# Turning a norm's rows with the root on a diagonal matrix, in a two-network fp32 kernel on one core

## The chip, the cores and the metric

The kernel runs on one core of one Trainium2 chip. The core has a matrix engine (TensorE, "PE" in the profile), a vector engine (VectorE, "DVE"), a scalar engine (ScalarE, "ACT"), a general engine (GpSimd, "POOL") and an engine that here only starts transfers (SyncE, "SP"). The metric is the device time of one execution in microseconds; the figure for a kernel is the median of several runs.

## The reference

Two small networks run one after the other on the same 256 rows x of 1024 fp32 numbers. What matters here are the norms and what they feed:

```python
def rmsnorm(x, g):
    y = x * lax.rsqrt(jnp.mean(x * x, axis=-1, keepdims=True) + RMS_EPS)
    return y * g

def first_block(x, mem, ...):
    for l in range(2):
        h = rmsnorm(x, norm_mix[l])
        (u_ssm, q_lat, kv_lat, k_rope, hg_q, ..., gate_logits) = jnp.split(h @ w_in[l], ...)
        y_ssm = s5_mixer(u_ssm, ...)
        y_mla = mla_mixer(q_lat, kv_lat, ...)   # rmsnorm(q_lat, q_norm) @ w_uq, rmsnorm(kv_lat, kv_norm) @ w_ukv
        y_hg = hgrn2_mixer(hg_q, ...)           # (rmsnorm(o, g_norm) per head * silu(gate)) @ w_o
        x = x + (gated sum of the three) @ w_out[l]
        x = x + memory_cross_attention(rmsnorm(x, norm_cross[l]), ...)
        x = x + swiglu_ffn(rmsnorm(x, norm_ffn[l]), ...)
    return rmsnorm(x, norm_final)

def second_block(x, c, ...):
    for layer in range(2):
        shift, scale, gate = jnp.split(silu(c) @ w_ada[layer] + b_ada[layer], 3, axis=-1)
        h = rmsnorm(x, norm_g[layer]) * (1.0 + scale) + shift
        y = even_mixer(h, ...) if layer == 0 else odd_mixer(h, ...)   # window and sparse attention; block attention
        x = x + gate * y
    return rmsnorm(x, final_g)
```

## The kernel before

The 256 rows are two row tiles of 128 partitions (t = 0, 1). Every weight is streamed from the chip's memory in pieces of 128x512 fp32 numbers (`piece`): SP starts the transfer into `raw`, ACT rounds it to the high part `whi` (L383), and DVE subtracts to get the low part `wlo` (L384). A product in full precision is then three products of a faster fp32 type (`mm3`, L389 to L391): high by high, high by low, low by high. The activations have to stand with their features on the partitions for that, and split in the same way. So `transT_into` turns 128x128 blocks on PE with an identity matrix (L486), four blocks to a bank of PE's output memory; ACT copies the bank out as the high part and DVE subtracts for the low part (L489).

A norm before (`norm`): ACT squares both halves of a row tile with a sum per row (L469, with a read of the accumulator), POOL adds the halves up with the scale 1/1024 (L452, L456) and raises the sum to the power -1/2 (L462); this number per row is called the root here. DVE multiplies the row by root and weight at once, in two halves (L500), and the eight blocks are turned. `normer` does this for the mixer's norm of the first network's second layer, for both cross attention norms and both feed-forward norms. `mla_lat` does it for the two latents of the MLA mixer (L622 with 256 columns, L633 with 512), and `hg_out` for four heads with four roots per row (L850 by the roots, L851 by the gate). The two norms of the second network also add a shift to all rows: L1523 in its second layer, and L1550 and L1553 in its first, which is worked together with the first network's last norm and therefore multiplies a row that was normed once by a second root (`rtb`). Shift and scale come from a small product, are written to memory, and are read back with a copy on every partition (`ada_row`).

The order on each engine is not written out by hand: a scheduler places the instructions by its own estimates of their lengths and by priorities. `residual`, which adds a product to x, works it so that row tile 0 ends first; the last pieces of the weight are kept for tile 1 (they are the ones named `B` or `E` beside `whi`), so PE works the kept products of tile 1 while tile 0's norm is made by the other engines. `high_priority` brings that norm forward.

Of the kernel before, what the change touches and what calls it, by code (L numbers as in the profile page):

```python
# [13 lines left out]
ALU = mybir.AluOpType  # L14
# [3 lines left out]
P = 128  # L18
NT = 2
D = 1024  # L20
# [183 lines left out]
class Net:  # L204
# [264 lines left out]
        self.nc.scalar.activation(j[:, :n], src, AF.Square, accum_out=s)  # L469
        return s  # L470

    def transT(self, src, kt, t, tag, scale=None, slots=None):
# [4 lines left out]
        self.transT_into(src, kt, hi, lo, 0, scale)  # L477
        return hi, lo

    def transT_into(self, src, kt, hi, lo, k_at, scale=None):  # L480
        nc = self.nc
        for b in range(0, kt, 4):
            nb = min(4, kt - b)
            pt = self.trb([P, 4, P])[:, :nb]
            for j in range(nb):
                nc.tensor.transpose(pt[:, j, :], src[:, (b + j) * P:(b + j + 1) * P], self.ident)  # L486
            h, l = hi[:, k_at + b:k_at + b + nb, :], lo[:, k_at + b:k_at + b + nb, :]
            if scale is None:
                self.last_turned = nc.scalar.copy(h, pt), nc.vector.tensor_sub(l, pt, h.bitcast(F32))  # L489
            else:  # L490
                nc.scalar.mul(h, pt, scale)
                nc.vector.scalar_tensor_tensor(l, pt, scale, h.bitcast(F32), op0=ALU.mult, op1=ALU.subtract)

    def norm(self, xt, g, out=None):
# [8 lines left out]
    def into(self, T, t, xn):  # L503

        if not T:
            T.extend(self.place_rows())
        self.transT_into(xn, 8, T[0][:, :, t, :], T[1][:, :, t, :], 0)

    def normer(self, name):

        g, T = self.bcast(name, D, "gbc"), []
        return T, lambda t: self.into(T, t, self.norm(self.xs[t], g))


    def sincos(self, ang, k, s, c, sign=1.0):
# [99 lines left out]
    def mla_lat(self, l, hT, gq, gkv):  # L615
        nc = self.nc
        S = {"knT": [], "kp": [], "qnT": [], "V": []}
        pk = self.proj(hT, f"wkv{l}", 0, 8, every=1)
        for t in range(NT):
            r = self.rstd([self.ssq(pk[t][:, :256], "ssqb")], 256, "rsk")  # L620
            kn = self.t([P, 512], "w2a", bufs=2)[:, :256]
            nc.vector.scalar_tensor_tensor(kn, pk[t][:, :256], r, gkv, op0=ALU.mult, op1=ALU.mult)  # L622
            S["knT"].append(self.transT(kn, 2, t, "mk", slots=(f"Q{2 * t}", f"Q{2 * t + 1}")))
            pe = self.t([P, 32], f"kpe{t}")
            tmp = self.t([P, 2, 16], "kpet", bufs=2)
            self.rope1(pe, pk[t][:, 256:272], pk[t][:, 272:288], self.mcos[:, t, :], self.msin[:, t, :],
                       (tmp[:, 0], tmp[:, 1]), pe[:, :16], pe[:, 16:])
            S["kp"].append(pe)
        pq = self.proj(hT, f"win{l}", 0, 8, every=1)
        for t in range(NT):  # L630
            r = self.rstd([self.ssq(pq[t], "ssqa")], 512, "rsq")
            qn = self.t([P, 512], "w2a", bufs=2)
            nc.vector.scalar_tensor_tensor(qn, pq[t], r, gq, op0=ALU.mult, op1=ALU.mult)  # L633
            S["qnT"].append(self.transT(qn, 4, t, "mq", slots=(f"H{2 * t}", f"H{2 * t + 1}")))
        return S

    def mla_qkv(self, l, S):
# [196 lines left out]
    def hg_out(self, S):  # L834
        nc = self.nc
        outT = []
        for t in range(NT):
            o = self.accb([P, 4, P])
            for h in range(4):
                A = S["A"][t, h // 2]  # L840
                nc.tensor.matmul(o[:, h, :], A[0][:, h % 2, :], S["V"][t][:, h * P:(h + 1) * P], start=True, stop=t == 0)
                if t == 1:
                    nc.tensor.matmul(o[:, h, :], A[1][:, h % 2, :], S["V"][0][:, h * P:(h + 1) * P], start=False, stop=True)
            ss = self.t([P, 4], "hss", bufs=2)
            jk = self.t([P, 512], "junk", BF16)
# [6 lines left out]
            self.dump(f"hg{t}", y)  # L852
            outT.append(self.transT(y, 4, t, "gT", slots=(f"H{6 + 2 * t}", f"H{7 + 2 * t}")))
        return outT


# [642 lines left out]
            yield  # L1499

    def ada_row(self, l, i, r):
        self.nc.sync.dma_start(r, self.adad[l][:, i * D:(i + 1) * D].partition_broadcast(P).rearrange("p o n -> p (o n)"))
        return r

    def ada_rows(self, l, shift, scale):

        nc = self.nc
        self.ada_row(l, 0, shift)
        self.ada_row(l, 1, scale)
        for c in range(2):  # L1510
            cols = slice(c * 512, c * 512 + 512)
            g = self.s(f"B{c}", [P, 512])
            nc.sync.dma_start(g, self.A[f"normg{l}"][:, cols].partition_broadcast(P).rearrange("p o n -> p (o n)"))
            nc.vector.scalar_tensor_tensor(scale[:, cols], scale[:, cols], 1.0, g, op0=ALU.add, op1=ALU.mult)
        self.ada_ready = shift, scale

    def norm_ada(self, l):
        shift, g = self.ada_ready
        out = []

        def then(t):
            xn = self.norm(self.xs[t], g)
            self.nc.vector.tensor_add(xn, xn, shift)  # L1523
            self.into(out, t, xn)

        return out, then

    def norm_ada2(self, l):

        nc = self.nc  # L1530
        shift, g = self.ada_ready
        gf = self.bcast("normf", D, "gbc")
        out, rs = [], []

        def then(t):
            x = self.xs[t]
            xn = self.t([P, D], "xn")
            cols = [slice(c * 512, c * 512 + 512) for c in range(2)]

            r, q = (self.t([P, 1], n, bufs=2) for n in ("rs", "rq"))  # L1540
            for i, c in enumerate(cols):
                nc.vector.tensor_mul(xn[:, c], x[:, c], gf[:, c])
                s, u = self.ssq(x[:, c], f"ssq{i}"), self.ssq(xn[:, c], f"ssu{i}")
                nc.gpsimd.tensor_scalar(r, s, 1.0 / D, r if i else EPS, op0=ALU.mult, op1=ALU.add)
# [336 lines left out]
```

## Time and profile before

| | us |
|---|---|
| median of 3 runs | 1493.55 |
| lowest and highest run | 1491.51 and 1494.88 |
| the profiled execution | 1489.82 |
| its span, first to last instruction | 1488.0 |
| PE busy | 1404.0 (94%) |
| DVE busy | 1097.8 (74%) |
| ACT busy | 823.9 (55%) |
| POOL busy | 51.7 (3%) |
| transfers, mean | 174 GB/s |

The busy time of PE includes a modelled tail of each product, so consecutive products overlap in it: two records that start 0.23 us apart may each be shown as 0.39 long. What a product costs is therefore read from the distance of starts. The granted clock of PE was 0.990 of full speed over the span. In the timeline a row's bracket tells how long its engine was idle before it, and which instruction ended that idle time.

### The profile page before, as it was taken

To read this page: it belongs to the slowest core of one execution; us is meant where nothing else is said; L and a number is where in the kernel's file an instruction comes from. 1 tells how busy PE (TensorE), PEld (TensorE's weight loads), DVE (VectorE), ACT (ScalarE), POOL (GpSimd) and SP (SyncE) were. 2 spreads that over 40 slices of the span, in tenths; PEclk is the share of its full clock that TensorE was granted. 3 is DMA by queue.
4 is the path that set the end of the run, shared out by engine and by line. 5 is a ranking of instruction groups with operands and counts; after the bars stand their busy time and mean duration, and the time that the engine had idled before them with its cause. 6 is when DMAs were issued, how large, how long until landed. Compare 5 with 4: busy or idle time off the path is not lost.

```text
span 1488.0 us, 28521 instructions
## 1 busy us (share of the span) xinstructions
PE 1404.0 (94%) x10148; PEld 1183.6 (80%) x10148; DVE 1097.8 (74%) x2287; ACT 823.9 (55%) x1789; POOL 51.7 (3%) x135
## 2 busy tenths in 40 slices
PE   6999899999999999989999999999999899999997
PEld 5788777878899977778777778789988687767776
DVE  7886987666598887567897776588885775677656
ACT  5575555556455555485556565555544455544564
POOL 1100001000000000100001000000000100000000
PEclk9999999999999999999999999999999999999999
DMA  5634344556488775432345566468887453445343
GB/s 188 191 118 129 103 156 157 190 177 195 133 291 276 258 236 180 159 116 87 116 142 178 190 208 193 147 208 263 288 261 235 127 172 100 131 147 171 119 130 107
DMA packets 150775, 259.45 MB, mean 174 GB/s; under 512 B 18424, under 2 KB 33960, under 8 KB 150632
## 3 DMA queue, kind: packets, MB, share of 16 engines
q1 hardware_dynamic: 145880, 254.59, 53.9%
q10 hardware_dynamic: 4464, 2.22, 0.5%
q8 instruction: 80, 1.31, 0.3%
q0 software_dynamic: 288, 0.81, 0.2%
q14 instruction: 63, 0.52, 0.1%
HBM read 254.77 MB, written 1.08 MB: 172 GB/s over the span
## 4 chain that ended last, share of the span: by engine, by line
PE 71%; DVE 11%; DMA 7%; ACT 6%; issue 3%; POOL 2%; ACTq 1%; SPq 0%; POOLq 0%; DVEq 0%
PE acc L389 16%; PE acc L390 16%; PE acc L391 16%; DVE wlo L384 2%; PE tr L390 2%; PE tr L389 2%; PE tr L391 2%; PE tr L486 2%; PE at L539 2%; ACT whi L383 2%; PE acc L599 1%; PE tr L568 1%; DMA raw<-in_win_dram 1%; PE tr L690 1%; DMA raw<-in_wout_dram 1%
## 5 line engine op out<-in xcount | busy, mean ns | idle before, releaser
L383 ACT CAST whi<-raw 128x512 fp32r<-128x512 f32 (+3 forms) x739 | 449.6, 615 | 379.9 <-PE acc L391 155.3
L384 DVE TENSOR_TENSOR wlo<-raw,whi 128x512 fp32r<-128x512 f32 (+3 forms) x739 | 493.0, 678 | 212.9 <-ACT whi L383 206.7
L390 PE MATMUL acc<-wlo,hTh 128*128 128x512 f32 (+3 forms) x588 | 231.8, 394 | 4.2 <-DVE wlo L384 4.1
L389 PE MATMUL acc<-whi,hTh 128*128 128x512 f32 (+3 forms) x588 | 229.1, 395 | 5.5 <-DVE gate L1235 2.5
L391 PE MATMUL acc<-whi,hTl 128*128 128x512 f32 (+3 forms) x588 | 229.1, 390 | 0.0
L389 PEld LDWEIGHTS acc<-whi,hTh 128*128 128x128 f32 x588 | 111.2, 190 | 31.3 <-DVE gate L1235 3.7
L390 PEld LDWEIGHTS acc<-wlo,hTh 128*128 128x128 f32 x588 | 112.1, 191 | 25.2 <-DVE wlo L384 6.2
L389 PE MATMUL acc<-hTh,whi 128*128 128x256 f32 x448 | 128.0, 286 | 0.0
L391 PEld LDWEIGHTS acc<-whi,hTl 128*128 128x128 f32 x588 | 111.9, 191 | 19.9
L391 PE MATMUL acc<-hTh,wlo 128*128 128x256 f32 x448 | 127.3, 285 | 0.0
L390 PE MATMUL acc<-hTl,whi 128*128 128x256 f32 x448 | 127.0, 284 | 0.0
L389 PE MATMUL tr<-hTh,whi 128*128 128x256 f32 x320 | 90.6, 283 | 0.0
L390 PE MATMUL tr<-hTl,whi 128*128 128x256 f32 x320 | 90.6, 283 | 0.0
L391 PE MATMUL tr<-hTh,wlo 128*128 128x256 f32 x320 | 90.5, 283 | 0.0
L389 PE MATMUL acc<-whi,H 128*128 128x512 f32 (+1 forms) x222 | 87.5, 396 | 1.5 <-ACT whi L383 1.3
L390 PE MATMUL acc<-wlo,H 128*128 128x512 f32 (+1 forms) x222 | 86.0, 387 | 0.7 <-DVE wlo L384 0.7
L389 PEld LDWEIGHTS acc<-hTh,whi 128*128 128x128 f32 x448 | 85.8, 191 | 0.9 <-issue 0.8
L391 PE MATMUL acc<-whi,H 128*128 128x512 f32 (+1 forms) x222 | 86.4, 389 | 0.0
L390 PEld LDWEIGHTS acc<-hTl,whi 128*128 128x128 f32 x448 | 85.8, 191 | 0.1
L391 PEld LDWEIGHTS acc<-hTh,wlo 128*128 128x128 f32 x448 | 85.7, 192 | 0.1
L557 ACT ACTIVATE prob<-at,mx 128x256 f32<-128x256 f32 (+1 forms) x128 | 53.5, 430 | 25.7 <-DVE mx L551 19.7
L391 PEld LDWEIGHTS tr<-hTh,wlo 128*128 128x128 f32 x320 | 61.4, 192 | 0.0
(514 smaller groups left out, 2785.7 us busy)
## 6 DMA issues: line engine op xcount, KB each, us to landing
raw<-in_win_dram SPq DMA_DIRECT2D x176, 256.0 KB, 3.2
raw<-in_wgu_dram SPq DMA_DIRECT2D x176, 256.0 KB, 3.8
raw<-in_wdn_dram SPq DMA_DIRECT2D x88, 256.0 KB, 3.4
raw<-in_wod_dram SPq DMA_DIRECT2D x64, 256.0 KB, 2.9
s5u<-in_wada_dram SPq DMA_DIRECT2D x48, 256.0 KB, 5.1
gate<-in_wada_dram SPq DMA_DIRECT2D x48, 256.0 KB, 4.6
raw<-in_wev_dram SPq DMA_DIRECT2D x40, 256.0 KB, 3.1
raw<-in_wglu_dram SPq DMA_DIRECT2D x32, 256.0 KB, 3.4
```

The costliest lines, as they stand in the source:

```text
L383: nc.scalar.copy(hi, raw)
L384: nc.vector.tensor_sub(lo, raw, hi)
L389: nc.tensor.matmul(ps, l[0], r[0], start=first, stop=False)
L390: nc.tensor.matmul(ps, l[0], r[1], start=False, stop=False)
L391: nc.tensor.matmul(ps, l[1], r[0], start=False, stop=last)
L486: nc.tensor.transpose(pt[:, j, :], src[:, (b + j) * P:(b + j + 1) * P], self.ident)
L539: nc.tensor.matmul(s[:, j, c], qT(h), kT(h)[:, c], start=not masks, stop=not masks or (j, k) == (hp - 1, nkt - 1))
L557: nc.scalar.activation(p[:, j, :], s[:, j, :], AF.Exp, bias=mx[:, j:j + 1], scale=scale, accum_out=den[:, hs[j]:hs[j] + 1])
L568: nc.tensor.transpose(pt[:, j * nkt + k, :], p[:, j, k * P:(k + 1) * P], self.ident)
L599: nc.tensor.matmul(o[a:a + 64, h, :], pts[:, j * nkt + k, a:a + 64], v(h, k), start=k == 0, stop=k == nkt - 1)
L690: self.nc.tensor.transpose(tp[:, j, :], src[:, j * w:(j + 1) * w], self.ident)
```

## The change

The root is no longer multiplied into the rows on DVE. Where the rows are turned, the second operand of the turning is not the identity but a diagonal matrix that carries the root of each row (`diag`: identity times the root, on DVE), and the turning is a plain fp32 product in place of a transpose. The weight (or the gate) is multiplied into the rows without the root, so this step no longer waits for POOL. A shift is added on PE, as a product of one row of shifts with one row of ones that starts the bank which the turned blocks are then added to; it is loaded on one partition only. The change covers `norm` (all large norms but the first layer's mixer norm, which is made elsewhere, and the last norm), the latent norms in `mla_lat`, the output norm in `hg_out` (four diagonals per row tile), and both norms with a shift.

```diff
+    def diag(self, r, d=None):
+        d = self.t([P, P], "diag", bufs=2) if d is None else d
+        self.nc.vector.tensor_scalar(d, self.ident, r, None, op0=ALU.mult)
+        return d
...
     def transT_into(...)
+            if shift is not None:
+                for j in range(nb):
+                    nc.tensor.matmul(pt[:, j, :], shift[0:1, cut(j)], self.cst("ones")[0:1].to_broadcast([1, P]), start=j == 0, stop=False)
             for j in range(nb):
-                nc.tensor.transpose(pt[:, j, :], src[:, (b + j) * P:(b + j + 1) * P], self.ident)
+                if by is None:
+                    nc.tensor.transpose(pt[:, j, :], src[:, cut(j)], self.ident)
+                else:
+                    nc.tensor.matmul(pt[:, j, :], src[:, cut(j)], by[b + j] if isinstance(by, list) else by,
+                                     start=shift is None, stop=shift is None or j == nb - 1)
...
     def norm(self, xt, g)
         s = [self.ssq(xt[:, c * 512:(c + 1) * 512], f"ssq{c}") for c in range(2)]
-        r = self.rstd(s, D, "rs")
-        xn = self.t([P, D], "xn") if out is None else out
+        xn = self.t([P, D], "xn")
         for c in range(2):
             cols = slice(c * 512, c * 512 + 512)
-            self.nc.vector.scalar_tensor_tensor(xn[:, cols], xt[:, cols], r, g[:, cols], op0=ALU.mult, op1=ALU.mult)
-        return xn
+            self.nc.vector.tensor_mul(xn[:, cols], xt[:, cols], g[:, cols])
+        return xn, self.diag(self.rstd(s, D, "rs"))
...
     mla_lat, the same for the 512 columns of q
-            nc.vector.scalar_tensor_tensor(kn, pk[t][:, :256], r, gkv, op0=ALU.mult, op1=ALU.mult)
-            S["knT"].append(self.transT(kn, 2, t, "mk", slots=(f"Q{2 * t}", f"Q{2 * t + 1}")))
+            nc.vector.tensor_mul(kn, pk[t][:, :256], gkv)
+            S["knT"].append(self.transT(kn, 2, t, "mk", slots=(f"Q{2 * t}", f"Q{2 * t + 1}"), by=self.diag(r)))
...
     hg_out
-            nc.vector.tensor_mul(y.rearrange("p (h d) -> p h d", h=4), o, self.bc(r, P))
-            nc.vector.tensor_mul(y, y, S["G"][t])
-            outT.append(self.transT(y, 4, t, "gT", slots=(f"H{6 + 2 * t}", f"H{7 + 2 * t}")))
+            nc.vector.tensor_mul(y, o.rearrange("p h d -> p (h d)"), S["G"][t])
+            d = [self.s(f"Q{2 + i}", [P, 2, P]) for i in range(2)]
+            by = [self.diag(r[:, h:h + 1], d[h // 2][:, h % 2]) for h in range(4)]
+            outT.append(self.transT(y, 4, t, "gT", slots=(f"H{6 + 2 * t}", f"H{7 + 2 * t}"), by=by))
...
     second layer of the second network
-            xn = self.norm(self.xs[t], g)
-            self.nc.vector.tensor_add(xn, xn, shift)
-            self.into(out, t, xn)
+            self.into(out, t, *self.norm(self.xs[t], g), shift)
...
     first layer of the second network
-            for i, c in enumerate(cols):
-                a = nc.vector.scalar_tensor_tensor(xn[:, c], xn[:, c], r2, g[:, c], op0=ALU.mult, op1=ALU.mult)
-                if i:
-                    self.here(a)
-                nc.vector.tensor_add(xn[:, c], xn[:, c], shift[:, c])
-            self.into(out, t, xn)
+            for c in cols:
+                nc.vector.tensor_mul(xn[:, c], xn[:, c], g[:, c])
+            self.into(out, t, xn, self.diag(r2), shift)
```

The scheduler places the new instructions. At the first cross norm, row tile 0, PE had this order before (`acc` is the bank of tile 1 that the kept products fill, `tr` the bank of the turning; each name ends in its buffer's number):

```order
L389 MATMUL acc_4013<-B_934_4019,H_806_3584 128x512
L390 MATMUL acc_4013<-B_935_4020,H_806_3584 128x512
L391 MATMUL acc_4013<-B_934_4019,H_807_3585 128x512
L389 MATMUL acc_4013<-whi_4040,H_872_3824 128x512
L486 MATMUL tr_4091<-cst_t,xn_4086 128x128 x4
L390 MATMUL acc_4013<-wlo_4041,H_872_3824 128x512
L486 MATMUL tr_4098<-cst_t,xn_4086 128x128 x4
L391 MATMUL acc_4013<-whi_4040,H_873_3825 128x512
```

and has this order with the change:

```order
L389 MATMUL acc_4031<-B_942_4037,H_814_3602 128x512
L390 MATMUL acc_4031<-B_943_4038,H_814_3602 128x512
L501 MATMUL tr_4111<-diag_4107,xn_4099 128x128 x4
L501 MATMUL tr_4118<-diag_4107,xn_4099 128x128 x4
L391 MATMUL acc_4031<-B_942_4037,H_815_3603 128x512
L389 MATMUL acc_4031<-whi_4058,H_880_3842 128x512
L390 MATMUL acc_4031<-wlo_4059,H_880_3842 128x512
L391 MATMUL acc_4031<-whi_4058,H_881_3843 128x512
```

The two groups of four turnings, which stood on both sides of a product, now follow each other directly, and stand after the second product with a kept piece, where before they stood two products later.

DVE's order at the same place before (`x_84` is a half of tile 0, `x_85` of tile 1, `gbc` the weight):

```order
L1295 TENSOR_TENSOR x_84<-x_84,acc_4000 128x512
L1295 TENSOR_TENSOR x_85<-x_85,acc_3911 128x512
L500 SCALAR_TENSOR_TENSOR xn_4086<-x_84,rsb_4084,gbc_3899 128x512 x2
L489 TENSOR_TENSOR hTl_4090<-tr_4091,hTh_4089 128x4x128
L489 TENSOR_TENSOR hTl_4090<-tr_4098,hTh_4089 128x4x128
```

and with the change:

```order
L1311 TENSOR_TENSOR x_84<-x_84,acc_4018 128x512
L516 TENSOR_TENSOR xn_4099<-x_84,gbc_3917 128x512
L1311 TENSOR_TENSOR x_85<-x_85,acc_3929 128x512
L475 TENSOR_SCALAR diag_4107<-cst_t,rsb_4105 128x128
L505 TENSOR_TENSOR hTl_4110<-tr_4111,hTh_4109 128x4x128
L516 TENSOR_TENSOR xn_4157<-x_85,gbc_3917 128x512
L505 TENSOR_TENSOR hTl_4110<-tr_4118,hTh_4109 128x4x128
```

The multiplication by the weight now stands ahead of the other tile's addition, the diagonal behind it, and the weight's multiplication of tile 1 comes between the low parts of tile 0.

At the first norm with a shift, row tile 0, PE before (`at` is tile 1's bank, `H` the turned operand):

```order
L390 MATMUL at_14095<-wlo_14594,H_2839_12113 128x512
L391 MATMUL at_14095<-whi_14593,H_2840_12114 128x512
L389 MATMUL at_14095<-whi_14602,H_2841_12115 128x512
L390 MATMUL at_14095<-wlo_14603,H_2841_12115 128x512
L391 MATMUL at_14095<-whi_14602,H_2842_12116 128x512
L389 MATMUL at_14095<-whi_14611,H_2841_12115 128x512
L486 MATMUL tr_14652<-cst_t,xn_14619 128x128 x4
L390 MATMUL at_14095<-wlo_14612,H_2841_12115 128x512
```

and with the change (`M` holds the shift, L496 are the products of the shift, here already those of tile 1):

```order
L389 MATMUL at_14151<-whi_14640,H_2865_12169 128x512
L390 MATMUL at_14151<-wlo_14641,H_2865_12169 128x512
L391 MATMUL at_14151<-whi_14640,H_2866_12170 128x512
L501 MATMUL tr_14708<-diag_14704,xn_14675 128x128 x4
L501 MATMUL tr_14719<-diag_14704,xn_14675 128x128 x4
L389 MATMUL at_14151<-whi_14649,H_2865_12169 128x512
L390 MATMUL at_14151<-wlo_14650,H_2865_12169 128x512
L391 MATMUL at_14151<-whi_14649,H_2866_12170 128x512
L389 MATMUL at_14151<-whi_14658,H_2867_12171 128x512
L496 MATMUL tr_14790<-cst_t,M_3255_14115 128x128 x4
L390 MATMUL at_14151<-wlo_14659,H_2867_12171 128x512
L496 MATMUL tr_14801<-cst_t,M_3255_14115 128x128 x4
L391 MATMUL at_14151<-whi_14658,H_2868_12172 128x512
```

The turnings of tile 0 stand four 512-column products earlier and are together; eight products of the shift, for the banks of tile 1, are new among the kept products (those for tile 0 stand further ahead).

## Rows read from the trace of the kernel before

**Rows 1.** Of the page: busy time and share by engine, and the chain's shares.
```profile
PE 1404.0 (94%) x10148; PEld 1183.6 (80%) x10148; DVE 1097.8 (74%) x2287; ACT 823.9 (55%) x1789; POOL 51.7 (3%) x135
...
PE 71%; DVE 11%; DMA 7%; ACT 6%; issue 3%; POOL 2%; ACTq 1%; SPq 0%; POOLq 0%; DVEq 0%
```

**Rows 2.** The waits of PE: awaited line, us in total, times, longest us.
```profile
PE tr L486 <- DVE xn L500: 6.3, 10, 0.8
...
PE tr L486 <- DVE xn L1553: 3.6, 2, 2.3
...
PE tr L486 <- DVE w2a L622: 2.3, 2, 1.8
PE tr L486 <- DVE xn L1523: 2.3, 2, 2.0
...
PE tr L486 <- DVE w2a L851: 2.0, 3, 1.2
...
PE acc L389 <- DVE w2a L850: 1.3, 1, 1.3
...
PE tr L486 <- DVE w2a L633: 1.0, 2, 0.8
```

**Rows 3.** The timeline at two stretches: start, us, engine, line, operation, count.
```profile
215.12 1.06 PE L841 MATMUL acc<-H,Q 128*128 128x128 f32 x8
...
1343.05 1.07 PE L486 MATMUL tr<-cst_t,xn 128*128 128x128 f32 x8 [0.26 <-DVE xn L1523]
```

**Rows 4.** Groups by line and shape: busy us, mean ns of one, idle before.
```profile
L500 DVE SCALAR_TENSOR_TENSOR xn<-x,rsb,gbc 128x512 f32<-128x512 f32 x20 | 14.1, 748 | 8.2 <-POOL rsb L462 8.2
...
L1372 PE MATMUL acc<-H,H 128*128 128x128 f32 x64 | 8.5, 281 | 0.0
...
L952 DVE TENSOR_SCALAR B<-B,cst_t 128x128 f32<-128x128 f32 x8 | 2.3, 283 | 1.4 <-DMA B<-in_ssmbc_dram 1.4
...
L1542 DVE TENSOR_TENSOR xn<-x,gbc 128x512 f32<-128x512 f32 x4 | 2.7, 688 | 0.1
```

**Rows 5.** The timeline of the first cross norm, first row tile.
```profile
328.96 0.19 ACT L469 ACTIVATION_READ_ACCUMULATOR junk<-x 128x1 f32 x1
...
329.32 0.26 POOL L456 TENSOR_SCALAR rs<-ssq,rs 128x1 f32<-128x1 f32 x1 [7.01 <-ACT junk L469]
...
329.67 0.55 POOL L462 TENSOR_TENSOR rsb<-rs,nhalf 128x1 f32<-128x1 f32 x1
...
329.94 0.39 PE L391 MATMUL acc<-B,H 128*128 128x512 f32 x1
...
330.17 0.40 PE L389 MATMUL acc<-whi,H 128*128 128x512 f32 x1
330.25 1.41 DVE L500 SCALAR_TENSOR_TENSOR xn<-x,rsb,gbc 128x512 f32<-128x512 f32 x2 [0.58 <-POOL rsb L462]
...
331.15 0.63 PE L486 MATMUL tr<-cst_t,xn 128*128 128x128 f32 x4 [0.58 <-DVE xn L500]
```

**Rows 6.** The timeline of the second shifted norm, first row tile.
```profile
1330.26 0.55 POOL L462 TENSOR_TENSOR rsb<-rs,nhalf 128x1 f32<-128x1 f32 x1
...
1332.78 1.22 DVE L1523 TENSOR_TENSOR xn<-xn,E 128x1024 f32<-128x1024 f32 x1
...
1334.05 1.09 PE L486 MATMUL tr<-cst_t,xn 128*128 128x128 f32 x8 [1.99 <-DVE xn L1523]
```

**Rows 7.** The timeline at a latent norm of the second layer.
```profile
615.32 0.48 DVE L622 SCALAR_TENSOR_TENSOR w2a<-acc,rskb,gate 128x256 f32<-128x256 f32 x1 [0.72 <-POOL rskb L462]
```

**Rows 8.** The timeline of DVE and POOL at the first shifted norm.
```profile
1175.10 1.29 DVE L384 TENSOR_TENSOR wlo<-raw,whi 128x512 fp32r<-128x512 f32 x2
1175.19 1.25 POOL L1544 TENSOR_SCALAR rs<-ssq,rs 128x1 f32<-128x1 f32 x1 [0.55 <-DVE B L384]
```

**Rows 9.** One stretch (busy us, counts, PEclk, DMA, GB/s), and the span's clock.
```profile
616.40:619.80 3.40, 3.40 (x11) 2.63 (x10) 2.21 (x11) 1.30 (x3) 0.00 (x0) 0.51 0.13 48
...
core 0: 1488.0 us, clock 0.990
```

More of the change, by code (lines that the diff above doesn't have):

```diff
@@ L470, in ssq, with transT @@
         return s
-    def transT(self, src, kt, t, tag, scale=None, slots=None):
+    def diag(self, r, d=None):
+        d = self.t([P, P], "diag", bufs=2) if d is None else d
+        self.nc.vector.tensor_scalar(d, self.ident, r, None, op0=ALU.mult)
+        return d
+    def transT(self, src, kt, t, tag, scale=None, slots=None, by=None):
         if slots:
@@ L476, in transT, with transT_into @@
             hi, lo = self.t([P, kt, P], f"{tag}h{t}", F32R), self.t([P, kt, P], f"{tag}l{t}", F32R)
-        self.transT_into(src, kt, hi, lo, 0, scale)
+        self.transT_into(src, kt, hi, lo, 0, scale, by)
         return hi, lo
-    def transT_into(self, src, kt, hi, lo, k_at, scale=None):
+    def transT_into(self, src, kt, hi, lo, k_at, scale=None, by=None, shift=None):
         nc = self.nc
@@ L484, in transT_into @@
             pt = self.trb([P, 4, P])[:, :nb]
+            cut = lambda j: slice((b + j) * P, (b + j + 1) * P)
+            if shift is not None:
+                for j in range(nb):
+                    nc.tensor.matmul(pt[:, j, :], shift[0:1, cut(j)], self.cst("ones")[0:1].to_broadcast([1, P]), start=j == 0, stop=False)
             for j in range(nb):
-                nc.tensor.transpose(pt[:, j, :], src[:, (b + j) * P:(b + j + 1) * P], self.ident)
+                if by is None:
[3 more added lines that the diff above has]
+                                     start=shift is None, stop=shift is None or j == nb - 1)
             h, l = hi[:, k_at + b:k_at + b + nb, :], lo[:, k_at + b:k_at + b + nb, :]
@@ L492, in transT_into, with norm, into @@
                 nc.vector.scalar_tensor_tensor(l, pt, scale, h.bitcast(F32), op0=ALU.mult, op1=ALU.subtract)
-    def norm(self, xt, g, out=None):
+    def norm(self, xt, g):
         s = [self.ssq(xt[:, c * 512:(c + 1) * 512], f"ssq{c}") for c in range(2)]
-        r = self.rstd(s, D, "rs")
-        xn = self.t([P, D], "xn") if out is None else out
+        xn = self.t([P, D], "xn")
         for c in range(2):
             cols = slice(c * 512, c * 512 + 512)
-            self.nc.vector.scalar_tensor_tensor(xn[:, cols], xt[:, cols], r, g[:, cols], op0=ALU.mult, op1=ALU.mult)
-        return xn
-    def into(self, T, t, xn):
+            self.nc.vector.tensor_mul(xn[:, cols], xt[:, cols], g[:, cols])
+        return xn, self.diag(self.rstd(s, D, "rs"))
+    def into(self, T, t, xn, by, shift=None):
         if not T:
             T.extend(self.place_rows())
-        self.transT_into(xn, 8, T[0][:, :, t, :], T[1][:, :, t, :], 0)
+        self.transT_into(xn, 8, T[0][:, :, t, :], T[1][:, :, t, :], 0, by=by, shift=shift)
     def normer(self, name):
         g, T = self.bcast(name, D, "gbc"), []
-        return T, lambda t: self.into(T, t, self.norm(self.xs[t], g))
+        return T, lambda t: self.into(T, t, *self.norm(self.xs[t], g))
     def sincos(self, ang, k, s, c, sign=1.0):
@@ L632, in mla_lat @@
             qn = self.t([P, 512], "w2a", bufs=2)
-            nc.vector.scalar_tensor_tensor(qn, pq[t], r, gq, op0=ALU.mult, op1=ALU.mult)
-            S["qnT"].append(self.transT(qn, 4, t, "mq", slots=(f"H{2 * t}", f"H{2 * t + 1}")))
+            nc.vector.tensor_mul(qn, pq[t], gq)
+            S["qnT"].append(self.transT(qn, 4, t, "mq", slots=(f"H{2 * t}", f"H{2 * t + 1}"), by=self.diag(r)))
         return S
@@ L849, in hg_out @@
             y = self.t([P, 512], "w2a", bufs=2)
-            nc.vector.tensor_mul(y.rearrange("p (h d) -> p h d", h=4), o, self.bc(r, P))
-            nc.vector.tensor_mul(y, y, S["G"][t])
-            self.dump(f"hg{t}", y)
-            outT.append(self.transT(y, 4, t, "gT", slots=(f"H{6 + 2 * t}", f"H{7 + 2 * t}")))
+            nc.vector.tensor_mul(y, o.rearrange("p h d -> p (h d)"), S["G"][t])
+            d = [self.s(f"Q{2 + i}", [P, 2, P]) for i in range(2)]
+            by = [self.diag(r[:, h:h + 1], d[h // 2][:, h % 2]) for h in range(4)]
+            outT.append(self.transT(y, 4, t, "gT", slots=(f"H{6 + 2 * t}", f"H{7 + 2 * t}"), by=by))
         return outT
@@ L1501, in ada_row @@
     def ada_row(self, l, i, r):
-        self.nc.sync.dma_start(r, self.adad[l][:, i * D:(i + 1) * D].partition_broadcast(P).rearrange("p o n -> p (o n)"))
+        n = r.shape[0]
+        self.nc.sync.dma_start(r, self.adad[l][:, i * D:(i + 1) * D].partition_broadcast(n).rearrange("p o n -> p (o n)"))
         return r
@@ L1507, in ada_rows @@
         nc = self.nc
+        shift = shift[0:1]
         self.ada_row(l, 0, shift)
```

## The prediction

> **What bounds the kernel now.** I read the busy table and the chain first [rows 1]. TensorE (PE) is busy 1404.0 of 1488.0 us, and it carries 71% of the chain that ended last; the vector engine (DVE) is busy for 74% and the scalar engine (ACT) for 55%. So PE's own work is the bound nearly everywhere: a product added to its queue costs its full length unless PE stood idle just before it. The second view is the list of what PE waits for [rows 2]. It gives the most that the change can win: PE's waits for tiles that need the root of a norm are 6.3 us before the turning of the large norms (10 waits, the longest 0.8), 3.6 and 2.3 us at the two norms with a scale and shift, 2.3 and 1.0 us at the two latent norms of the MLA mixer, and 2.0 and 1.3 us at the HGRN2 output norm. The sum is 18.8 us. Third, I looked at single places in time, for prices and for what follows the root there.
>
> **What is added on PE.** Eight turnings of 128x128 blocks by the identity span 1.07 us; four plain fp32 products of the same size, with two records each, span 1.06 us [rows 3]. The modelled tail of a record is in both spans, so I take differences. A plain product's record alone is 0.281 us (L1372) [rows 4], and the 7 other records then take 0.113 us each in the first span and 0.111 in the second. A turning costs 0.113 us, a plain product 2 x 0.111 = 0.222. The changed turning is a plain product with the diagonal, so each block costs 0.11 us more.
>
> The blocks, counted in the code: the five large norms of the first network, 2 row tiles of 8 blocks each, 80; the two norms with scale and shift, 32; the latent norms, 2 layers with 2 tiles of 2 and 4 blocks, 24; the HGRN2 output, 2 layers with 2 tiles of 4 blocks, 16. That is 152, and 152 x 0.11 = 16.7 us. The shift takes 8 products per tile with a contraction of 1, at 2 tiles and 2 norms, so 32. The trace has no product of that shape; its bounds are a turning's 0.113 and a plain product's 0.222. I take 0.222, since the operands are plain fp32 with 128 columns: 7.1 us. Together PE gets 23.8 us more work (20.3 at the low bound).
>
> **What is removed, and what is late next.** On DVE the fused multiplication by root and weight, 0.748 us for 512 columns, becomes a multiplication of 0.688 that needs no root, and a diagonal. A 128x128 multiplication by a number per partition took 0.283 us (L952) [rows 4], so the diagonal takes 0.28, and DVE's total changes little. What becomes shorter is the time from the root to the turning.
>
> *Large norms.* At the first cross norm the square's accumulator is read at 328.96, POOL scales it at 329.32 and raises it to the power at 329.67 (0.55 us), the fused multiplication starts at 330.25, and the turning at 331.15 after an idle of 0.58 us [rows 5]. With the diagonal, 0.28 us stand where 0.75 stood (the first half), so the block is ready 0.47 us earlier. But in the new order its products stand two 512-column products ahead of where the turnings stood, and such products follow each other at 0.23 us (329.94 to 330.17), 0.46 in all. The wait stays at about 0.57 us there: POOL's two steps are what is late next. At other norms the move is 2 to 11 products. Ten waits at 0.47 would give 4.7 of the 6.3 us, none if each moves forward by as much; I take 2.0.
>
> *The two norms with scale and shift.* In the second layer the power ends at 1330.81, the shift's addition alone is 1.22 us, and the turning at 1334.05 had waited 1.99 us, from 1332.06 on [rows 6]. A diagonal is ready at about 1331.1, before PE is free, and its products do not stand far enough ahead to bring the wait back. The first layer's two waits end on the same kind of addition (L1553). Of 3.6 + 2.3 us I take 4.4 as given back, three quarters.
>
> *The latent norms.* The diagonal takes 0.28 us against the 0.48 of L622 [rows 7], and against 0.75 at L633, which has the form of L500. Two waits of each are in the list: 2 x 0.2 + 2 x 0.47 = 1.3 us given back.
>
> *The HGRN2 output.* Four diagonals a tile, 4 x 0.28 = 1.1 us, follow the root where two multiplications of 0.69 (the form of L1542) followed it, so the turning's wait shrinks by 0.3 us at most. The bank, though, is now read without the root, so the 1.3 us for L850 goes: 1.6 us.
>
> Given back in all: 2.0 + 4.4 + 1.3 + 1.6 = 9.3 us. Net: 23.8 - 9.3 = +14.5 us. The transfer of the shift becomes one row in place of 128 copies of it, and some issues on ACT's queue move back in the S5 stage; PE waits for neither now, and I put both at nothing, covered by PE's own products. If that cover is too short, a late S5 operand would be a new wait of the order of those listed, 1 to 2 us.
>
> **A rule that speaks against multiplying "meanwhile".** At 1175.19 a POOL step on 128x1 took 1.25 us, while the like one at the cross norm took 0.26 [rows 5]; beside the first, DVE subtracted two pairs of tiles from 1175.10 on for 1.29 us, and the two ended within 0.05 us [rows 8]. So POOL stood still for about 1 us. The Trainium skill, in "SBUF — State Buffer", section "Who interferes with whom", says that a vector instruction with two inputs in that memory and a GpSimd read share one port pair, as an exclusive lock for the whole instruction; the trace agrees.
>
> The new multiplication has two such inputs, and it stands between the square and the diagonal, where POOL works. If it held POOL up at each of the 14 tiles of the large norms by its 0.69 us, that would be 9.7 us on PE; at the other end, nothing. At the cross norm the multiplication (0.69) starts with the Square (0.63), and the accumulator's read (0.19) follows before POOL is asked [rows 5], so it is over. I take 0 and keep 9.7 as the upper end.
>
> **Sum.** The profiled execution took 1489.82 us, its span 1488.0; +14.5 gives 1504.3 for it. The median of the three runs is 1493.55, 3.7 above the profiled one, so the forecast for the median is 1493.55 + 14.5 = 1508. Bounds: all 18.8 us of waits given back, +5.0 or 1498.6 (at the low price of the shift +1.5, 1495.1); nothing given back, +23.8 or 1517.4.
>
> **The rivals.** *All the waits go (1498.6).* For it: no wait is longer than 2.3 us, and every one is on a tile that now needs less behind its root. Against it: the root itself is late at the large norms, and the products were moved ahead.
>
> *Nothing is given back, and POOL is held up (+23.8 to +33.5, so 1517 to 1527).* For it: the lock above, and the places two to eleven products earlier. Against it: the long additions of the shift are certain to go.
>
> *The clock's low stretches go too (faster).* PE's clock was granted at half, the 1.2 of the two levels 1.2 and 2.4 GHz, from 616.4 to 619.8 us: 0.51 over that stretch. Just before it L622 ended, at 615.8 [rows 7], for which PE had waited 1.8 us [rows 2]. Over the span the mean is 0.990, so at most 1% of 1488, about 15 us, is lost to the clock [rows 9]. If all of it went with the waits, 18.8 + 15 against 23.8 would make -10, so 1483.6. It decides only when more than 23.8 us come back, that is, all the waits and a third of what the clock takes. Against it: the one wait seen ahead of such a stretch is shortened by just 0.2 us.
>
> **How the numbers follow.** I give +10 to +20 around the forecast 0.50; nearly all waits gone (+3 to +10) 0.21; nothing given back or POOL held up 0.10; the rest, 0.19, is the fast side, where the waits, other stages or the clock give back nearly all, or more, of what PE is given. What this kernel's runs can tell from no change is 0.2%, about 3 us. Of the fast side I put 0.10 within that and 0.09 below it. So faster 0.09, same 0.10, slower 0.81. The range goes from 1494, near the low bound of "all waits gone", to 1518, where nothing is given back; the likeliest case's own range is 1503.5 to 1513.5.
>
> **What would show it.** In the profile after, PE's busy time should be higher by 20 to 25 us, with two records for each turned block, and four products with the diagonal should span 1.06 us; if they span 0.6, the price is wrong and the sum turns. PE's waits for diagonals should add up to about 4 us at the large norms and to less than 2 at the two shifted norms. POOL's steps L452 and L456 should stay at 0.2 to 0.5 us; at 0.9 and more the lock has struck. Shift products at 0.113 would lower the sum by 3.5 us. A total below 1496.5 would mean that PE's added work was not what set the end.

## The result, and the profile of the changed kernel

The changed kernel took 1513.1 us (median of 4 runs, 1510.92 to 1515.45) against 1492.53 us of the kernel before (4 runs, 1487.06 to 1494.88): ratio 1.0144, 95% interval 1.0124 to 1.0164. A second measurement beside later experiments gave 1.0161 (1.0123 to 1.0199). So it is slower by 20.6 us where +14.5 was forecast; the 1513.1 lies in the range of 1494 to 1518 and inside the likeliest case's own range by 0.4 us. The second ratio would make it 1516.6 us, outside that narrower range. The profiled execution took 1515.04 us, its span 1513.2, 25.2 more than before; its mean granted clock was 0.988 against 0.990.

The page's busy times and the chain's shares, as in [rows 1]:

```profile
PE 1437.5 (95%) x10364; PEld 1213.6 (80%) x10364; DVE 1099.7 (73%) x2315; ACT 824.9 (55%) x1789; POOL 53.4 (4%) x135
...
PE 75%; DVE 9%; ACT 5%; DMA 5%; issue 3%; POOL 1%; ACTq 1%; SPq 0%; POOLq 0%; DVEq 0%
```

PE is busy 33.5 us longer, in 216 records more (152 for the turnings, 64 for the shift), and carries more of the chain; DVE, ACT and POOL did not move by 2 us. What PE waits for, as in [rows 2] (L475 makes the diagonal, `Q` are the four of an HGRN2 tile):

```profile
PE tr L501 <- DVE diag L475: 11.8, 15, 1.8
...
PE tr L501 <- DVE Q L475: 1.3, 3, 0.6
```

The 18.8 us that stood in seven rows are 13.1 us now. The first cross norm, the stretch of [rows 5], with the products two matmuls earlier in PE's queue than the turnings were:

```profile
333.23 0.27 POOL L456 TENSOR_SCALAR rs<-ssq,rs 128x1 f32<-128x1 f32 x1 [7.01 <-ACT junk L469]
...
333.58 0.55 POOL L462 TENSOR_TENSOR rsb<-rs,nhalf 128x1 f32<-128x1 f32 x1
...
334.17 0.28 DVE L475 TENSOR_SCALAR diag<-cst_t,rsb 128x128 f32<-128x128 f32 x1 [0.60 <-POOL rsb L462]
...
334.60 2.02 PE L501 MATMUL tr<-diag,xn 128*128 128x128 f32 x16 [0.59 <-DVE diag L475]
...
336.38 0.48 PE L391 MATMUL acc<-B,H 128*128 128x512 f32 x1
```

The step from the power to the turning is shorter: 334.17 to 334.60, where the fused multiplication had taken 330.25 to 331.15. The wait is 0.59 us all the same, where 0.57 was worked out. Eight products, 16 records, stand from 334.60 to 336.38: 0.111 us a record, the price that was taken from [rows 3].

### The profile page after: what moved, and what is told of

It is laid out like the page before. It is cut to its first block, busy times and chain, and to the rows that moved or that the text cites. A ratio compares the mean times of both kernels' runs of the same rounds, so it can differ in the third digit from the quotient of the medians.

```text
span 1513.2 us, 28970 instructions
## 1 busy us (share of the span) xinstructions
PE 1437.5 (95%) x10364; PEld 1213.6 (80%) x10364; DVE 1099.7 (73%) x2315; ACT 824.9 (55%) x1789; POOL 53.4 (4%) x135
## 4 chain that ended last, share of the span: by engine, by line
PE 75%; DVE 9%; ACT 5%; DMA 5%; issue 3%; POOL 1%; ACTq 1%; SPq 0%; POOLq 0%; DVEq 0%
PE acc L389 17%; PE acc L390 17%; PE acc L391 17%; PE tr L501 2%; PE tr L390 2%; PE tr L389 2%; PE tr L391 2%; DVE wlo L384 2%; PE at L555 2%; PE tr L584 1%; PE acc L615 1%; DMA raw<-in_win_dram 1%; ACT whi L383 1%; PE tr L499 1%; DMA raw<-in_wout_dram 1%
## 5 line engine op out<-in xcount | busy, mean ns | idle before, releaser
L391 PE MATMUL acc<-whi,hTl 128*128 128x512 f32 (+3 forms) x588 | 229.6, 391 | 0.0
L391 PEld LDWEIGHTS acc<-whi,hTl 128*128 128x128 f32 x588 | 112.5, 191 | 20.4
L391 PE MATMUL acc<-hTh,wlo 128*128 128x256 f32 x448 | 127.3, 285 | 0.0
L391 PE MATMUL tr<-hTh,wlo 128*128 128x256 f32 x320 | 90.5, 283 | 0.0
L391 PE MATMUL acc<-whi,H 128*128 128x512 f32 (+1 forms) x222 | 87.3, 393 | 0.0
L391 PEld LDWEIGHTS acc<-hTh,wlo 128*128 128x128 f32 x448 | 85.7, 192 | 0.1
L390 PEld LDWEIGHTS tr<-hTl,whi 128*128 128x128 f32 x320 | 61.4, 192 | 0.0
```

The source lines that it names most:

```text
L390: nc.tensor.matmul(ps, l[0], r[1], start=False, stop=False)
L391: nc.tensor.matmul(ps, l[1], r[0], start=False, stop=last)
```

## The experiments

All ratios are to the kernel before, measured beside it. Each run also lists its span and the mean granted clock of PE; their product is what the span would be with the clock at full speed throughout, as far as PE bounds it. It is a mean over the runs, with a 95% interval of 1 to 2.6 us to either side, and it separates work from clock. Where all of PE's waits are summed, the sum is over one trace of each kernel (75.0 us before).

| kernel | ratio (95% interval) | mean clock | span x clock, us |
|---|---|---|---|
| before (23 runs; 1472.2 to 1472.7 in the other measurements) | 1 | 0.987 | 1472.4 |
| changed, first and second measurement | 1.0144 (1.0124-1.0164), 1.0161 (1.0123-1.0199) | 0.987, 0.9845 | 1491.7, 1492.3 |
| e1 no shift | 1.0040 (1.0021-1.0059) | 0.9896 | 1482.5 |
| e2 shift last, one row | 1.0145 (1.0111-1.0180) | 0.9838 | 1490.0 |
| e9 shift last, 128 rows | 1.0105 (1.0070-1.0139) | 0.9875 | 1489.2 |
| e12 shift strewn, 128 rows | 1.0087 (1.0059-1.0116) | 0.9867 | 1486.2 |
| e3 plain product with the identity | 1.0093 (1.0065-1.0121) | 0.988 | 1488.4 |
| e5 large norms only | 1.0064 (1.0045-1.0083) | 0.9865 | 1481.3 |
| e6 latent and HGRN2 norms only | 1.0025 (1.0010-1.0040) | 0.9877 | 1476.4 |
| e7 shifted norms only | 1.0092 (1.0058-1.0125) | 0.9842 | 1481.6 |
| e8 no weight | 1.0170 (1.0143-1.0198) | 0.9835 | 1492.3 |
| e4 root on DVE | 0.9964 (0.9946-0.9982) | 0.9868 | 1467.2 |
| e10 root on DVE and ACT | 0.9964 (0.9945-0.9983) | 0.9865 | 1467.2 |

**The price of a turning (e3).** Only this in `transT_into` of the kernel before, at the 152 blocks:

```diff
-                nc.tensor.transpose(pt[:, j, :], src[...], self.ident)
+                nc.tensor.matmul(pt[:, j, :], src[...], by, start=True, stop=True)   # by = self.ident
```

> The kernel before with one difference: at the 152 changed blocks the turning is a plain fp32 product with the identity in place of a transpose. No diagonal, no step moved, the root multiplied on DVE as before. Theory A (a block costs 0.11 us more on a PE that is the bound): 152 x 0.11 = 16.7 us slower than before, about 1509, ratio 1.011. Rival (the plain product's second half lies in the waits around a norm): at most half of that, 1501 or less, ratio 1.0055.

1508.33 us, +0.93% or 13.9 us (9.7 to 18.1); +16.0 in span x clock. The 16.7 us lie in the interval, the rival's half does not. The page:

```profile
PE 1424.0 (94%) x10300; PEld 1206.0 (80%) x10300; DVE 1099.3 (73%) x2287; ACT 825.9 (55%) x1789; POOL 52.8 (3%) x135
```

PE's busy time rose by 20.0 us with 152 records more. The products do not hide in the waits around a norm.

**The shift (e1, e2).** e1 drops the shift's products, so that its result lacks the shift; e2 issues them behind the four turnings of their bank. This is e2's edit:

```diff
-            if shift is not None:
-                for j in range(nb):
-                    nc.tensor.matmul(pt[:, j, :], shift[0:1, ...], ones[1 row], start=j == 0, stop=False)
             for j in range(nb):
-                    nc.tensor.matmul(pt[:, j, :], src[...], by, start=shift is None, stop=...)
+                    nc.tensor.matmul(pt[:, j, :], src[...], by, start=shift is None or j == 0, stop=shift is None)
+            if shift is not None:
+                for j in range(nb):
+                    nc.tensor.matmul(pt[:, j, :], shift[0:1, ...], ones[1 row], start=False, stop=j == nb - 1)
```

> The changed kernel without the products of the shift; the shift is left out of the result. Theory A (PE's added work sets the time, and the shift's 64 records cost more than their own length, because they stand in small groups among 512-column products of another type: 10.0 us of their own and about 2.5 on the neighbours): 12 to 13 us faster than the changed kernel, so about 1500.5, ratio to the kernel before 1.005. Theory B (they cost 7.1 us as predicted, and the rest of the loss is in waits or in POOL being held up): about 1506, ratio 1.009.

> The changed kernel with the shift's products behind the turnings of the same bank, so that the scheduler keeps them together with these. Same products, same count. Theory A (the change of product type costs when the shift's products are strewn among others): 4 to 5 us faster than the changed kernel, about 1508.5, ratio to before 1.0107. Theory B (only their own length counts): no change, 1513, ratio 1.014; a small loss if the strewn ones lay in waits.

e1 took 1500.07 us, less than the changed kernel by 13.0 us of the medians, or by 1.04 points and 15.5 us of the ratios. That is theory A's 12 to 13 us or more, and not theory B's 7. In span x clock it is 9.2 us (9.8 against the second measurement), and the rest is clock: e1 has the highest of all. e2 came out against theory A and at theory B's number (1516.15 us, no gain). Its trace shows what else changed. PE in e2, first shifted norm, tile 0 (start, duration, line, operation, tile, count; four products are eight records), and the window behind it (length, busy us and counts of PE, its weight loads, DVE, ACT, POOL; then PE's granted clock, DMA share, GB/s):

```profile
1182.63 1.16 PE L498 MATMUL tr<-diag,xn 128*128 128x128 f32 x8 [1.65 <-DVE diag L475]
1183.72 1.74 PE L502 MATMUL tr<-cst_t,M 1*128 1x128 f32 x8
1185.38 2.08 PE L498 MATMUL tr<-diag,xn 128*128 128x128 f32 x8
1187.39 2.07 PE L502 MATMUL tr<-cst_t,M 1*128 1x128 f32 x8
1189.39 0.80 PE L389 MATMUL at<-whi,H 128*128 128x512 f32 x1
```

```profile
1184.10:1194.30 10.20, 10.20 (x35) 8.46 (x35) 5.53 (x10) 3.58 (x7) 1.01 (x2) 0.50 0.39 114
```

Of the 32 records of turnings and shift, the first turnings take 1.09 us; then the clock falls to half, 1.2 of 2.4 GHz, for 10.2 us, and the next groups take 1.7 to 2.0 us each. By span x clock bunching saved 1.7 to 2.3 us of work, which is within the error of these means, and the time shows none of it. So "strewn or not" was not the whole cause, and what the shift's products have of their own, one row in the contraction, came under suspicion.

**One row or 128 (e9, e12).** The shift's row stands on top of 127 rows of zeros, against ones; records and order stay the same (e9 on e2, e12 on the changed kernel):

```diff
-        shift = shift[0:1]
-        self.ada_row(l, 0, shift)
+        nc.gpsimd.memset(shift, 0.0)
+        self.ada_row(l, 0, shift[0:1])
...
-    nc.tensor.matmul(pt[:, j, :], shift[0:1, cut(j)], self.cst("ones")[0:1].to_broadcast([1, P]), ...)
+    nc.tensor.matmul(pt[:, j, :], shift[:, cut(j)], self.cst("ones").to_broadcast([P, P]), ...)
```

> As e2_shift_last, but each product of the shift contracts over all 128 rows: the shift's row and 127 rows of zeros (set by POOL), against ones. The same records in the same order and of the same length. Theory C (the clock is lowered around the shifted norms because the products of the shift use one row of the array): the mean granted clock returns from 0.984 to 0.987 or 0.988, and the time falls from 1516 to about 1510, ratio to before 1.010 to 1.0115. Rival (what lowers it is the long run of small plain products without a 512-column product, whatever their rows): as e2_shift_last, 1.0145.

> The changed kernel in its own order, the shift's products strewn among others as there, but each contracting over 128 rows (one of the shift, 127 of zeros) in place of one. Theory D (what the shift costs above its length comes from the change between products of one row and of 128, and from the low clock that goes with them, not from the strewing): as e9_shift_full_rows, ratio to before 1.0095 to 1.0115, about 1509.5, clock 0.987; the product behind such a group starts 0.11 us after its last record, not 0.20. Rival (the strewing itself costs): 1.0125 to 1.0165 as the changed kernel.

e9: 1510.76 us, ratio 1.0105, clock 0.9875, at theory C's numbers, though the 0.40 points between e2 and e9 have an uncertainty of 0.49. The stretch that answers to e2's:

```profile
1184.86 1.16 PE L498 MATMUL tr<-diag,xn 128*128 128x128 f32 x8 [1.52 <-DVE diag L475]
1185.86 1.06 PE L502 MATMUL tr<-cst_t,M 128*128 128x128 f32 x8
1186.75 1.05 PE L498 MATMUL tr<-diag,xn 128*128 128x128 f32 x8
1187.64 1.06 PE L502 MATMUL tr<-cst_t,M 128*128 128x128 f32 x8
1188.46 0.48 PE L389 MATMUL at<-whi,H 128*128 128x512 f32 x1
```

```profile
1184.80:1195.00 10.20, 10.05 (x59) 8.57 (x59) 9.14 (x16) 5.45 (x13) 2.95 (x6) 1.00 0.51 151
```

The same 32 records take 3.6 us where e2 needed 6.8, at a clock of 1.00. At tile 1, where e2's clock was 1.00 too, they take 3.57 us in e9 (1196.16 to 1199.73) and 4.31 in e2 (1198.63 to 1202.94), 0.37 us more for each of the two groups of the shift. Over both norms that is 8 groups and 3.0 us; span x clock differs by only 0.8, while PE's waits sum to 69.3 us in e9's trace and to 66.2 in e2's, which is about the rest.

e12: 1509.08 us, ratio 1.0087 (upper end 1.0116, below the changed kernel's lower end). Here the work can be compared at full clock, record by record. First the changed kernel, the four products of the shift for tile 0's second bank and their neighbours; then e12 at the same place:

```profile
1174.14 0.40 PE L391 MATMUL acc<-whi,H 128*128 128x512 f32 x1
1174.47 0.71 PE L496 MATMUL tr<-cst_t,M 1*128 1x128 f32 x4
1175.11 0.49 PE L389 MATMUL acc<-whi,H 128*128 128x512 f32 x1
1175.53 0.48 PE L496 MATMUL tr<-cst_t,M 1*128 1x128 f32 x2
1175.94 0.51 PE L390 MATMUL acc<-wlo,H 128*128 128x512 f32 x1
1176.38 0.48 PE L496 MATMUL tr<-cst_t,M 1*128 1x128 f32 x2
1176.79 0.50 PE L391 MATMUL acc<-whi,H 128*128 128x512 f32 x1
```

```profile
1174.33 0.40 PE L391 MATMUL acc<-whi,H 128*128 128x512 f32 x1
1174.56 0.61 PE L496 MATMUL tr<-cst_t,M 128*128 128x128 f32 x4
1174.92 0.48 PE L389 MATMUL acc<-whi,H 128*128 128x512 f32 x1
1175.24 0.38 PE L496 MATMUL tr<-cst_t,M 128*128 128x128 f32 x2
1175.38 0.47 PE L390 MATMUL acc<-wlo,H 128*128 128x512 f32 x1
1175.69 0.38 PE L496 MATMUL tr<-cst_t,M 128*128 128x128 f32 x2
1175.83 0.48 PE L391 MATMUL acc<-whi,H 128*128 128x512 f32 x1
```

From the L391 ahead to the L391 behind it is 2.65 us with one row and 1.50 with 128. With one row a 512-column product starts 0.41 us behind the start of a two-record group, with 128 rows 0.14; and a group starts 0.33 to 0.44 us behind the product ahead of it instead of 0.23 to 0.32. Counted from the group's last record (records stand 0.11 us apart) the next product starts after 0.30 us with one row and 0.03 with 128, where 0.20 and 0.11 had been expected. So one row costs about 0.1 us ahead of a group and 0.27 behind it, and in the two traces this is the same for groups of 2, 4, 6, 8 and 16 records. The 64 records of the changed kernel stand in 15 groups: 15 x 0.37 = 5.6 us. The tile's name says what differs: `1*128` among `128*128`. The Trainium skill, "TensorEngine Tiling (Array Packing)", section "Key Properties", states that changing the tiling mode drains TensorE. The later starts would agree with that if a product of one row is another mode, which no run shows.

Theory D holds: its one row cost the changed kernel 5.4 to 6.1 us in span x clock, as the 15 groups add up to, and 8.5 to 11 us in time by the ratios. The strewing alone costs nothing: with 128 rows the strewn products (e12, 1486.2) even come out 3.0 us below the bunched ones (e9, 1489.2), with PE's waits at 67.0 us in all against 69.3. With one row, the strewing set how many groups there are.

**The parts alone (e5, e6, e7).** The kernel with the change at some sites only, the other sites as before (the edit is the diff shown above, in part).

> The change at the five large norms of the first network alone (80 blocks, no shift); all other norms as before. Theory A (PE pays 0.11 us a block, and the waits at these norms are not given back, since they were 6.3 us before and are 6.8 in the changed kernel): 6 to 9 us slower than before, ratio 1.004 to 1.006. Rival (the early multiplication pays for the products here, as the prediction's 2 us and a better order might): at most 3 us slower, ratio 1.002 or less.

> The change at the latent norms and the HGRN2 output norm alone (40 blocks). Theory A: 40 x 0.11 = 4.4 us on PE, less 3.2 us of waits that are gone in the changed kernel, so about 1 us slower, ratio 1.000 to 1.0015. Rival (the waits are only moved to the next product): 3 to 4 us slower, 1.0025.

> The change at the two norms with a shift alone (32 blocks and the 32 products of the shift). Theory A (the shift's products cost 9 to 11 us and not 7.1, and low stretches of the clock come with them): 3.5 + 10 - 2.7 = 11 us slower, up to 4 more by the clock, ratio 1.007 to 1.010. Rival (as predicted, 3.5 + 7.1 - 4.4 = 6.2): ratio 1.004. With e5 and e6 the three should add up to the whole change's 1.0144.

e5: 1504.67 us, 1.0064, just above theory A's upper end; the +9.0 us in span x clock are the price of 80 blocks, 8.8 us. e6: 1497.68 us, 1.0025, the rival's value; its interval excludes a gain and theory A's lower half, and the +4.1 us in span x clock are nearly the whole price of 40 blocks, 4.4 us. e7: 1505.8 us, 1.0092, theory A, with a clock of 0.9842. The sum of the three is 1.0181, with an uncertainty of 0.4 points, against 1.0144 and 1.0161. PE's waits for a diagonal in e5, e6 and e7:

```profile
PE tr L501 <- DVE diag L475: 6.8, 10, 0.9
```

```profile
PE tr L501 <- DVE diag L475: 1.9, 1, 1.9
...
PE tr L501 <- DVE Q L475: 1.4, 3, 0.6
```

```profile
PE tr L501 <- DVE diag L475: 1.5, 2, 1.1
```

At the large norms the 6.3 us of [rows 2] are 6.8: nothing came back. At the latent and HGRN2 norms 6.6 became 3.3. The rival's reason for e6's time, waits that move to the next product, does not show in its trace: all of PE's waits went from 75.0 to 71.5 us. Why e6 is slower by nearly the whole price all the same stays open. At the shifted norms 5.9 became 1.5 when they were changed alone, but 3.2 in the whole change (1.18, 0.78, 0.40 and 0.83).

**The multiplication "meanwhile" (e8, e4, e10).** e8 gives the product with the diagonal x itself and so leaves the weight out of the result:

```diff
-            self.nc.vector.tensor_mul(xn[:, cols], xt[:, cols], g[:, cols])
-        return xn, self.diag(self.rstd(s, D, "rs"))
+        return xt, self.diag(self.rstd(s, D, "rs"))
```

> The changed kernel with the weight left out at the five large norms and at the second norm with a shift, so that the rows go to the product with the diagonal as they are: 24 multiplications of 0.69 us on DVE are gone. Theory A (PE is the bound, the multiplication stands off its path and does not hold POOL up): within 2 us of the changed kernel, about 1512, ratio to before 1.0125 to 1.0145. Rival (the two-input multiplication holds up POOL or other work of DVE): 4 to 8 us faster, ratio 1.009 to 1.0115.

1520.51 us, ratio 1.0170. It is not faster, so the rival falls; it is beyond theory A's upper end too, and by span x clock (1492.3 against 1491.7 and 1492.3) it is the changed kernel, at a clock of 0.9835. POOL was held up in places all the same. DVE, POOL and PE at the first shifted norm of the changed kernel, whose multiplication e8 keeps (the last row is cut by the window's end):

```profile
1182.49 0.68 DVE L1566 TENSOR_TENSOR xn<-xn,M 128x512 f32<-128x512 f32 x1
1182.55 0.75 POOL L1561 TENSOR_SCALAR rq<-ssu,rq 128x1 f32<-128x1 f32 x1 [0.17 <-ACT junk L469]
...
1183.75 0.55 POOL L462 TENSOR_TENSOR rtb<-ru,nhalf 128x1 f32<-128x1 f32 x1
...
1184.34 0.28 DVE L475 TENSOR_SCALAR diag<-cst_t,rtb 128x128 f32<-128x128 f32 x1 [1.17 <-POOL rtb L462]
...
1184.68 1.49 PE L501 MATMUL tr<-diag,xn 128*128 128x128 f32 x11 [1.18 <-DVE diag L475]
```

POOL's L1561 takes 0.75 us there beside a multiplication of two tiles (a like step, L456, 0.27 at the cross norm), and is on the way to this diagonal; over the span POOL is busy 1.7 us more than before. In e8 it is busy 2.3 us less (51.1), and no time is gained. e4 keeps the early multiplication and the transposes, and puts the root (and the shift with it) on DVE (the edit in short):

```diff
-            self.nc.vector.scalar_tensor_tensor(xn[:, cols], xt[:, cols], r, g[:, cols], op0=ALU.mult, op1=ALU.mult)
+            self.nc.vector.tensor_mul(xn[:, c], xt[:, c], g[:, c])          # before the root is there
+            self.nc.vector.tensor_scalar(x, x, r, None, op0=ALU.mult)       # large and latent norms
+            self.nc.vector.scalar_tensor_tensor(x, x, r, shift, op0=ALU.mult, op1=ALU.add)   # with a shift
```

> The kernel before with the weight multiplied before the root is there, as in the change, but the root applied afterwards on DVE (with the shift in the same instruction), and the turnings left as transposes. Theory A (the loss is all on PE; an early multiplication by the weight does no harm): 3 to 8 us faster than before, 1485 to 1490, ratio 0.995 to 0.998. Rival (the two-input multiplication holds POOL up before the root): as slow as before or slower, 1493 to 1500, with POOL's steps L452 and L456 at 0.7 us and more.

> As e4_root_dve, but at the large norms the second half's root is multiplied on ACT beside the first half on DVE. Theory A (the turning's wait at a large norm is set by POOL's two steps and by the first half alone): no change to e4_root_dve, ratio to before 0.995 to 0.998. Rival (the second half is late): 1 to 3 us faster than e4_root_dve, ratio 0.9945 or less.

Both are faster than the kernel before: 1488.75 and 1489.32 us, ratio 0.9964 with intervals below 1. DVE's two forms in e4 (count, busy us, mean ns, idle before), and PE's waits:

```profile
L507 DVE TENSOR_SCALAR xn<-xn,rsb 128x512 f32<-128x512 f32 x20 | 8.8, 483 | 8.2 <-POOL rsb L462 8.2
...
L509 DVE SCALAR_TENSOR_TENSOR xn<-xn,rtb,M 128x512 f32<-128x512 f32 x4 | 2.8, 748 | 2.9 <-POOL rtb L462 2.9
```

```profile
PE tr L486 <- DVE xn L509: 7.3, 4, 2.6
PE tr L486 <- DVE xn L507: 6.8, 10, 0.8
...
PE tr L486 <- DVE kpet L617: 1.9, 1, 1.9
...
PE tr L486 <- DVE w2a L862: 0.8, 2, 0.6
...
PE acc L389 <- DVE w2a L620: 0.2, 1, 0.2
```

The multiplication by a number per row takes 0.483 us for 512 columns (the estimate had no such row), against 0.748 for the fused one. PE's waits at the large and the shifted norms did not fall (14.1 us against 12.2 in [rows 2]); those at the latent and HGRN2 norms did, from 6.6 to 2.9 us (L617, L862, L620; L617 is a step of the rotary part that DVE works at the latent norm's place). In all that is 1.8 us of the 5. The rest lies at other places: all of PE's waits went from 75.0 to 68.1 us. Which part of the edit shortened them no run separates. POOL's L452 and L456 on `rs` stay at 0.28 and 0.35 us on average, so the rival falls. e10 adds nothing, so the second half was not late.

> The changed kernel itself beside the others, for the mean of its granted clock and for its ratio on this chip. Theory C: the clock at 0.985 to 0.987, since its shift's products are strewn and not in one run; ratio 1.0125 to 1.0165.

1518.93 us, 1.0161, as theory C had it, and clock 0.9845, just under its 0.985; these are the second values of "changed" in the table.

## Why the prediction was right, and where its size was off

- *PE is the bound and the added products set the sign*: shown. e3 alone, which adds nothing but the second record, costs 13.9 us (16.0 at constant clock) against 16.7 in the sum, and without the shift the change is still slower (e1). The sign named for it, PE busy 20 to 25 us longer, came out at 33.5 (26.9 in e12, whose shift has 128 rows).
- *The shift, 7.1 us*: the term that was mis-sized. Its products were priced by their columns, as plain ones, and the trace of before had none with one row. With 128 rows they cost about that or less (e12 less e1: 3.7 in span x clock, 0.47 points or 7.0 us in time); with one row they cost 9 to 10 in span x clock (changed less e1), and in time 13 us by the medians or 15.5 by the ratios. In the stretch shown, three 512-column products of 0.23 us taken off, a product of the shift costs (2.65 - 0.69) / 4 = 0.49 us with one row and (1.50 - 0.69) / 4 = 0.20 with 128. The bounds of 0.113 and 0.222 were those of products of another height. What lay outside them is the 0.37 us for each group.
- *Waits given back, 9.3 us*: 5.7 at the places named (18.8 to 13.1). Large norms: 2.0 forecast, -0.5 measured. At the cross norm the scheduler put the products as far forward as the diagonal came earlier, as worked out (0.57, measured 0.59). None of the ten waits became shorter by more than 0.01 us, and taking 2.0 was the error. Shifted norms: 4.4 forecast, 2.7 measured. Latent norms: 1.3 forecast, 1.5 measured (3.3 to 1.8). HGRN2: 1.6 forecast, 2.0 measured (3.3 to 1.3). All of PE's waits went from 75.0 to 66.2 us (67.2 in the second trace of the changed kernel), so 8.8 came back, 3.1 of them at places that the prediction did not name. That the total comes near its 9.3 is luck, and no run separates why those other waits became shorter.
- *POOL held up by the multiplication, 0 taken*: the lock shows (0.75 us for L1561), but 1.7 us of POOL time in all, and e8 found nothing to gain. As the sign asked, L452 and L456 on `rs` stay low, at 0.31 and 0.37 us on average (0.26 and 0.36 before), though a single L456 takes 1.23 us (1.32 before). The 0 was nearly right.
- *The sum*: 16.7 + 7.1 + 5.6 for the one row - 8.8 of all waits = 20.6 at full clock; span x clock says 19.3 and 19.6. Against the forecast's 14.5 that is 5 us of work, the one row's; what is left of the measured loss is clock. That the first measurement stayed within the likeliest case's range by 0.4 us is luck too.
- *The rival of all waits gone* and *the fast side* did not come: 13.1 us of waits remain, and the clock's low stretches did not go, they grew around the shifted norms. Between 1150 and 1390 us the clock was at half for 3.4 us in the trace of before and for 10.2 and 23.8 us in the two traces of the changed kernel.

## What to carry to other kernels

Where the matrix engine is busy for 94% of the time, a step moved onto it is paid nearly in full (e3), and the waits it is to shorten are worth their sum at most; a scheduler that moves the consumer forward can take even that back, as at the ten large norms here. A multiplication by a number per row takes 0.483 us for 512 columns on the vector engine, which is busy for 74%; a second pass of the turning takes about as long (four blocks of 0.11 us), but on the bound engine. With the weight split from the root and both left on the vector engine, the shift in the same instruction, the kernel became 0.36% faster (e4); no run separates the two. A product with one row in its contraction was cheaper at full height, with zeros, where it stands among full products (e12); if it has to have one row, the fewer groups the better, at about 0.37 us each.

## What the runs showed of the hardware

- A group of 1x128 products among 128x128 and 128x512 ones costs its neighbours, at the same granted clock of 1.00: it starts 0.33 to 0.44 us behind a 512-column product instead of 0.23 to 0.32, and the next product starts 0.41 us behind the start of a two-record group instead of 0.14. That is about 0.37 us a group, whatever its length.
- The granted clock depends on what stands there: in e2, with 16 of 32 records on one row, it fell to 0.50 for 10.2 us at the first shifted norm, behind the first eight records of turnings, and with the same records on 128 rows (e9) it stayed at 1.00. Each is one execution. In the two traces of the changed kernel, one fell among this norm's shift products (0.50 from 1175.5 to 1185.5 us) and the other stayed at 1.00 there. A low stretch of 10.2 us stands at a shifted norm in four of the five traces with one row (e2, e7, e8, e11), and in none of the nine others, where the longest there is 6.8 us (e6). Over the runs the mean is 0.9844 for the 27 with one row and 0.9871 for the 12 of e9 and e12. That one row makes low stretches more frequent is therefore likely; what in it does so no run separates.
